# A hybrid decoder layer on one core: row scale into class order earlier, a pair's second turn later in its step, three weight tiles split in halves in other steps

## Chip, cores and metric

The kernel runs on one core of a Trainium2 chip. The metric is the device time of one execution in microseconds (us), as the median of several runs. Five engines work side by side, each through its own list of instructions in order: TensorE (PE, with its weight loads shown as PEld), VectorE (DVE), ScalarE (ACT), GpSimd (POOL) and SyncE (SP), which issues the DMAs here. An instruction that needs another engine's result waits on a semaphore, and what stands behind it on its engine waits with it.

## What is computed

One decoder layer on 1024 tokens of width 1024, in float32: attention over eight heads beside a gated recurrence over four heads, one output projection, and a feed-forward block.

```python
h = rmsnorm(x, mix_pre_norm[layer])
proj = h @ w_in[layer]
q_a, k_a, v_a, q_h, f_h, i_h, g_h = jnp.split(proj, splits, axis=-1)
attn = dilated_mixture_attention(q_a.reshape(ahead), k_a.reshape(ahead), v_a.reshape(ahead), slopes)
attn = rmsnorm(attn.reshape(B, S, ATTN_WIDTH), attn_out_norm[layer])
rec = hgrn2_recurrence(q_h, f_h, i_h, g_h, lower_bounds[layer], hgrn_out_norm[layer])
mixed = jnp.concatenate([attn, rec], axis=-1) @ w_out[layer]
x = x + rmsnorm(mixed, mix_post_norm[layer])
h = rmsnorm(x, mlp_pre_norm[layer])
ff = jnp.square(jax.nn.relu(h @ w_ff1[layer])) @ w_ff2[layer]
x = x + rmsnorm(ff, mlp_post_norm[layer])
```

The attention mixes three patterns with dilations 1, 4 and 16. The kernel therefore orders the tokens of a block by their class modulo 4 (`DIL = 4`) where it gathers keys by stride.

## The kernel before

Every matrix product runs in three passes (`three_pass`, L89 to L92): each operand is split into a rounded part `h` and a remainder `l`, and the products hh, hl and lh are added up in one PSUM bank. So each weight tile of 128 x 1024 must be split before use. `w_split` (L110) does it whole: ACT writes the rounded part (L86, or L124 with a gain for the output projection) and DVE the remainder (L87 or L125). `wo_half` (L132) does one half of 512 columns of an output tile (L140 on ACT, L141 on DVE); its second half also issues the next weight load on SP (L107). `w_get(i, ahead)` splits tiles in order until tile `i + ahead` is done. The raw tiles have two buffers, so a load can go out only when a split has freed one. The output projection has eight tiles, `WO0` to `WO0 + 7`; the first two take slabs of their own (tag S and BT, L179), the next two the ordinary weight buffers.

The order of the work is written out by hand: each engine executes its instructions in the order in which the Python code issues them. Projections are generators in a queue; `fill` (L195) takes units from it, mostly one contraction step of three matmuls of 128 x 512, and so sets the projections between the steps of the other work.

Two stretches matter here.

**The last recurrence heads and the first attention projections.** `rrow` (L253, 128 x 1024) holds the row scale of the first norm along the tokens, the same on all partitions. The recurrence heads use it in token order: `hgrn_qf` (L417) multiplies the projected q (L428) and the forget gate (L443) with it, for each half `hf` of 512 tokens, and then makes the gate's products (L444 to L452). The attention uses it in class order (L717, L781, L800). Between the two, ACT brings each half into class order with two copies, one with a strided read into a half-width buffer `rc` (L774) and one back (L775). Before, both pairs stand in `attn_proj(0)` (L758), each two contraction steps into the query projection of its half; the split of the next weight tile (`w_get` at `n == 4` of the first half) comes between them. The projection units of one recurrence head run inside `hgrn_core` (L484) of the head before: with the last gate products (L443 to L452) go the output sums of that head (L626 to L631), whose root POOL takes (L82, L83) before DVE applies the gate (L642). In the last head's core, the level loop multiplies keys and queries by running products (L580, L582 on DVE), and the next level's TensorE product `pl` (L576) reads them. Half-width buffers (tag `half`) come two at a time.

**The 64 attention steps.** The loop at L1326 makes eight steps for each of eight heads: four near blocks D0 to D3, two far pieces F0, F1, two pieces N0, N1. In a step, exponentials are taken on ACT (`raise_`, L936), the next scores are made (`look`), the step's weights are turned by TensorE transposes into a PSUM bank of tag t (`turn`, pt_D, pt_F, pt_N) and split from there by ACT and DVE (L975, L976), some projection units are filled in, the weights of the step before are multiplied with the values (`weigh`, pov), results are added up (`finish`, L1046), a key job follows in some steps (`key_job`, L736 on ACT, L737 on POOL), and then `hooks` (L1294) run what a step has of its own. More projection units end the step. Two heads make a pair. A finished pair's output is turned to token order in two parts: `pair_turn` (L1069) makes four transposes into a t bank (pot), and `pair_rows` (L1077) scales them out of the bank on DVE (L1079). The first part stands at the end of steps 17, 33 and 49, the second in steps 18, 34 and 50, with its transposes right behind the step's own `turn`. There are two banks of tag t.

The splits of the first output tiles stand at steps 42 (tile one, at the end of the step), 44 (tile two), 45 (tile three), 48 and 49 (tile four in halves). `row_turn` (L1146, transposes pmt, splits emt at L86 and L87) prepares token rows for the output projection, and from step 47 on `early_out` (L1173 on, product pwe) fills the projection units.

Of the kernel before, what the change touches and what calls it, by code (L numbers as in the profile page):

```python
# [11 lines left out]
AF = mybir.ActivationFunctionType  # L12
# [13 lines left out]
AH = 8  # L26
HH = 4
LEVELS = (1, 2, 4, 8, 16, 32, 64)
DIL = 4
# [3 lines left out]
def f32(ap):  # L33
    return ap.bitcast(F32)
# [3 lines left out]
def hymba_layer(ctx, tc, x, w_in, w_out, w_ff1, w_ff2, g_pre, lb_logits, g_mix, g_post,  # L38
                g_mlp, g_mlp_post, bias_tab, level_masks, ident_in, fold_in, out):
    nc = tc.nc  # L40
    V, S, G, TE = nc.vector, nc.scalar, nc.gpsimd, nc.tensor
# [18 lines left out]
    def half(name, dtype=F32):  # L60
        return sp.tile([P, 512], dtype, tag="half", name=name, bufs=2)
# [86 lines left out]
    def w_get(i, ahead=1):  # L148
        while done[1] < min(i + 1 + ahead, len(stream)):
            w_split()  # L150
        return parts[i]
# [26 lines left out]
    WO0 = len(stream)  # L178
# [13 lines left out]
    queue = []  # L192
# [17 lines left out]
    def drain():  # L210
        while queue:
            n = len(queue)
            fill(1e9)
            assert len(queue) < n or not queue
# [27 lines left out]
    for c in range(2):  # L242
        sl = slice(c * 512, c * 512 + 512)
# [150 lines left out]
    def classes(ap):  # L394
        return ap.rearrange("p (m r) -> p r m", r=DIL)
# [21 lines left out]
    def hgrn_qf(h):  # L417
        hd = heads[h]
        box = [None]
        w = w_get(4 * h + 2)  # L420
        qt = hd["qt"] = slab("S", f"qt{h}")
        sig = slab("P", f"sig{h}")
        for hf in range(2):
            sl = slice(hf * 512, hf * 512 + 512)
            yield from proj_t(w, f"q{h}", hf, box)
            if h == 0:
                row_scale(hf)
            V.tensor_tensor(out=qt[:, sl], in0=box[0], in1=rrow[:, sl], op=ALU.mult)  # L428
            S.activation(sig[:, sl], qt[:, sl], AF.Sigmoid)
            V.tensor_tensor(out=qt[:, sl], in0=qt[:, sl], in1=sig[:, sl], op=ALU.mult)  # L430
            yield 650.0
        w = w_get(4 * h + 3, 0)
        hd["prod"] = prod = [slab("BT", f"pr{q}{h}", F32R) for q in "hl"]
        kt = hd["kt"] = slab("S", f"kt{h}")
        tot = hd["tot"] = slab("S", f"tot{h}")
        for hf in range(2):
            sl = slice(hf * 512, hf * 512 + 512)
            for n, cost in enumerate(proj_t(w, f"f{h}", hf, box)):
                if hf == 0 and n == 3:
                    w_get(4 * h + 3, 2 if h + 1 < HH else 1)  # L440
                yield cost
            fr = half(f"fr{h}{hf}")
            V.tensor_tensor(out=fr, in0=box[0], in1=rrow[:, sl], op=ALU.mult)  # L443
            S.activation(tot[:, sl], fr, AF.Sigmoid)  # L444
            S.activation(kt[:, sl], fr, AF.Sigmoid, scale=-1.0)
            V.tensor_scalar(tot[:, sl], tot[:, sl], omlb[:, h:h + 1], lb[:, h:h + 1], op0=ALU.mult, op1=ALU.add)
            V.tensor_scalar(kt[:, sl], kt[:, sl], omlb[:, h:h + 1], None, op0=ALU.mult)
            full = half(f"pr{h}{hf}")
            V.tensor_tensor(out=full, in0=qt[:, sl], in1=kt[:, sl], op=ALU.mult)
            S.activation(prod[0][:, sl], full, AF.Copy)  # L450
            V.tensor_tensor(out=qt[:, sl], in0=qt[:, sl], in1=tot[:, sl], op=ALU.mult)
            V.tensor_tensor(out=prod[1][:, sl], in0=full, in1=f32(prod[0][:, sl]), op=ALU.subtract)  # L452
            yield 650.0

    def quarter_sets(hd, h, step, tots):

# [301 lines left out]
    def attn_proj(pr):  # L758
        stacks = [{}, {}]
        box = [None]  # L760
        while pr > 1 and not second_done[pr - 2]:
            yield None
        w = w_get(A0 + 3 * pr, 0)
        for hf in range(2):
            sl = slice(hf * 512, hf * 512 + 512)
            for n, cost in enumerate(proj_t(w, f"aq{pr}", hf, box)):
                if hf == 0 and n == 3 and turn_later:
                    values_turn()
                    cost += 450.0
                if hf == 0 and n == 4:  # L770
                    w_get(A0 + 3 * pr)
                if pr == 0 and n == 2:
                    moved = half(f"rc{hf}")
                    S.activation(moved.rearrange("p (r m) -> p r m", r=DIL), classes(rrow[:, sl]), AF.Copy)  # L774
                    S.activation(rrow[:, sl], moved, AF.Copy)  # L775
                yield cost
            if hf == 0:
                for i in range(2):
                    stacks[i]["q"] = slab("S", f"q{pr}_{i}", F32R)
            full = half(f"qf{pr}{hf}")  # L780
            V.scalar_tensor_tensor(full.rearrange("p (r m) -> p r m", r=DIL), classes(box[0]), -0.125,  # L781
                                   rrow[:, sl].rearrange("p (r m) -> p r m", r=DIL), op0=ALU.mult, op1=ALU.mult)
            lo = half(f"ql{pr}{hf}", F32R)
            for i, (a, b) in enumerate(halves):
                src = full[a:b].rearrange("p (r j i) -> p j r i", r=DIL, i=32)
                S.activation(by_class(stacks[i]["q"][a:b, sl]), src, AF.Copy)  # L786
                G.tensor_tensor(out=by_class(lo[a:b]), in0=src, in1=by_class(f32(stacks[i]["q"][a:b, sl])), op=ALU.subtract)  # L787
            nc.sync.dma_start(out=f32(stacks[0]["q"][64:128, sl]), in_=f32(lo[0:64]))
            nc.sync.dma_start(out=f32(stacks[1]["q"][0:64, sl]), in_=f32(lo[64:128]))
            yield 650.0  # L790
        wv = w_get(A0 + 3 * pr + 1, 0)
        vs = None

        def values(hf):
            for n, cost in enumerate(proj_t(wv, f"av{pr}", hf, box)):
                if n == 4:
                    w_get(A0 + 3 * pr + 1 + hf)
                yield cost
            full = half(f"vf{pr}{hf}")
            V.tensor_tensor(out=by_class(full), in0=in_blocks(box[0]),  # L800
                            in1=rrow[:, hf * 512:hf * 512 + 512].rearrange("p (r j i) -> p j r i", r=DIL, i=32), op=ALU.mult)
            turn_later.append((pr, vs, full, hf))
            yield 650.0

        vs = slab("V8", f"v{pr}", F32R, (P, NT, 2, 2, 64))
        yield from values(0)
        while pr > 0 and not first_done[pr - 1]:
            yield None
        wk = w_get(A0 + 3 * pr + 2, 0)
        for i in range(2):  # L810
            stacks[i]["kh"] = slab("S", f"kh{pr}_{i}", F32R)
            stacks[i]["kl"] = slab("S", f"kl{pr}_{i}", F32R)
        pairs[pr] = (stacks, vs)
        for hf in range(2):
            for n, cost in enumerate(proj_t(wk, f"ak{pr}", hf, box)):
                if n == 3 and hf == 0:
                    values_turn()
                    cost += 450.0
                yield cost
            keys_read(pr, box[0], hf)  # L820
            if hf == 0 and pr == AH // 2 - 1:
                early_rows()
            yield 650.0
        yield from values(1)
# [9 lines left out]
    def load_bias(hd):  # L834
        if hd < AH and hd not in bts:
            bts[hd] = slab("BT", f"bt{hd}") if hd < AH - 1 else early["table"][:, 0]
            nc.sync.dma_start(out=bts[hd][:, :NEAR + FAR], in_=table_dram[hd])
# [257 lines left out]
    NE = 4  # L1095
# [14 lines left out]
    def early_sums():  # L1110
        early["sum"] = [wide.tile([P, 2, D], F32, tag="A", name=f"esum{q}") for q in range(NE // 2)]
# [173 lines left out]
    for h in range(HH):  # L1285
# [10 lines left out]
        1: lambda: last_gate(1),  # L1296
        2: lambda: last_gate(2),
        3: lambda: last_gate(3),
        44: lambda: w_get(WO0 + 1, 0),
        45: lambda: w_split(),  # L1300
        46: lambda: row_turn(0, 0, tag="s"),
        47: lambda: [drain(), early_sums(), queue.extend(early_out(t) for t in range(NE))],
        48: lambda: [values_turn("t"), wo_half(3, 0)],
        49: lambda: [wo_half(3, 1), load_bias(AH - 1)],
        50: lambda: row_turn(1, 0),
        52: lambda: row_turn(2, 0),
        54: lambda: row_turn(3, 0),
        55: lambda: [wo_half(4, 0), row_load(0)],
# [17 lines left out]
    for s in range(n_steps):  # L1326
# [14 lines left out]
        if i == 2:  # L1341
            joint(hd, 0)
            spread_low(hd, 1)
        kind, g = ITEMS[i]
        turn(hd, kind, g)
        raise_(*coming, which=(1,))
        if s % 16 == 2 and s > 16:
            pair_turn(s // 16 - 1, 1)
        if kind != "D" or g % 2:
            to_weigh.append((hd, kind, g // 2 if kind == "D" else g))  # L1350
        units = UNITS[hd][i]
# [5 lines left out]
        for *w, r in last_fold:  # L1357
            finish(*w, *r)
        if s % 16 == 2 and s > 16:
            pair_rows(s // 16 - 1, 1)  # L1360
        if i == 0:
            far_queries(hd)
# [4 lines left out]
            send(hd)  # L1367
        elif i == 6:
            receive(hd)
        if s == 42:  # L1370
            w_get(WO0, 0)
        if i in (1, 2, 3, 6, 7):
            key_job()
        hooks.get(s, lambda: None)()
# [913 lines left out]
```

## Time and profile before

| | |
|---|---|
| median of three runs | 1212.91 us (1212.48 to 1214.87) |
| the profiled execution | 1212.77 us, its span 1211.0 us |
| granted TensorE clock | 0.999 |
| DMA, share of 16 engines | 43.8% |
| L774, class copy with strided read, 128 x 512 | 1.09 to 1.16 us, two of them |
| L775, copy back | 0.63 us, two of them |
| L124, whole output tile on ACT | 1.13 to 1.15 us |
| L140, half an output tile on ACT | 0.71 to 0.72 us |
| L141, the same half on DVE | 0.75 us |
| L1079, a pair's half scaled out of its bank | 0.68 to 0.69 us, six of them |

The span is the time from the first to the last instruction of the profiled execution; what lies around it belongs to the measured time as well. In the timeline a row gives the start and the duration in us, then engine, line, operation and tiles (out<-in); a bracket gives the engine's idle time before the instruction and what ended it. Instructions overlap a little at their ends, so the time that one holds its engine is best read from start to start.

### The profile page before, as it was taken

To read this page: it belongs to the slowest core of one execution; us is meant where nothing else is said; L and a number is where in the kernel's file an instruction comes from. 1 tells how busy PE (TensorE), PEld (TensorE's weight loads), DVE (VectorE), ACT (ScalarE), POOL (GpSimd) and SP (SyncE) were. 2 spreads that over 40 slices of the span, in tenths; PEclk is the share of its full clock that TensorE was granted. 3 is DMA by queue.
4 is the path that set the end of the run, shared out by engine and by line. 5 is a ranking of instruction groups with operands and counts; after the bars stand their busy time and mean duration, and the time that the engine had idled before them with its cause. 6 is when DMAs were issued, how large, how long until landed. Compare 5 with 4: busy or idle time off the path is not lost.

```text
span 1211.0 us, 17270 instructions
## 1 busy us (share of the span) xinstructions
PE 1197.1 (99%) x6338; PEld 1025.0 (85%) x6338; DVE 854.5 (71%) x1436; ACT 548.9 (45%) x1073; POOL 306.9 (25%) x288
## 2 busy tenths in 40 slices
PE   9999999999999999999999999999999999999997
PEld 8898989888888887888888888888888888888886
DVE  5697878776666767676689566766688554478796
ACT  7633333332565667765664222222234543534562
POOL 0121212021221211144330886575631000000022
PEclk9999999999999999999999999999999999999999
DMA  5222323123545456173514555554587534533337
GB/s 219 69 69 83 94 86 94 50 82 76 148 92 126 113 129 167 42 238 125 191 61 157 182 187 196 196 188 143 202 320 268 203 98 146 162 100 104 105 105 278
DMA packets 87667, 172.38 MB, mean 142 GB/s; under 512 B 14624, under 2 KB 40224, under 8 KB 87584
## 3 DMA queue, kind: packets, MB, share of 16 engines
q1 hardware_dynamic: 87584, 171.29, 43.8%
q8 instruction: 50, 0.82, 0.3%
q14 instruction: 33, 0.27, 0.1%
HBM read 116.98 MB, written 47.99 MB: 136 GB/s over the span
## 4 chain that ended last, share of the span: by engine, by line
PE 75%; ACT 1%; DVE 1%; issue 1%; POOL 0%; DVEq 0%; POOLq 0%; ACTq 0%
PE f L2028 18%; PE f2s L2028 7%; PE pwo L90 2%; PE pwo L92 2%; PE pwo L91 2%; PE pm_ak L90 1%; PE pm_av L90 1%; PE pm_ak L92 1%; PE pm_ak L91 1%; PE pm_av L92 1%; PE pm_av L91 1%; PE pm_aq L90 1%; PE pl L576 1%; PE pm_aq L92 1%; PE pm_aq L91 1%; PE pov L994 1%
## 5 line engine op out<-in xcount | busy, mean ns | idle before, releaser
L87 DVE TENSOR_TENSOR al<-ar,ah 128x1024 fp32r<-128x1024 f32 x56 | 70.6, 1261 | 80.9 <-ACT ah L86 78.6
L2028 PE MATMUL f<-bh,ah 128*128 128x512 f32 x320 | 124.5, 389 | 0.0
L2028 PE MATMUL f<-bl,ah 128*128 128x512 f32 x320 | 124.5, 389 | 0.0
L2028 PE MATMUL f<-bh,al 128*128 128x512 f32 x320 | 124.5, 389 | 0.0
L86 ACT ACTIVATE ah<-ar 128x1024 fp32r<-128x1024 f32 x56 | 59.2, 1057 | 86.0 <-DMA ar<-actd 85.7
L2028 PEld LDWEIGHTS f<-bh,ah 128*128 128x128 f32 x320 | 60.1, 188 | 12.6
L2028 PEld LDWEIGHTS f<-bl,ah 128*128 128x128 f32 x320 | 60.1, 188 | 12.5
L2028 PEld LDWEIGHTS f<-bh,al 128*128 128x128 f32 x320 | 60.1, 188 | 12.3
L2102 POOL TENSOR_SCALAR lbl<-ssq 128x1 f32<-128x1 f32 x4 | 3.3, 820 | 245.8 <-ACT fd L2098 245.6
L1651 POOL TENSOR_TENSOR e<-x,e 128x512 f32<-128x512 f32 x14 | 21.6, 1540 | 131.0 <-DVE x L1602 131.0
L2028 PE MATMUL f2s<-bh,al 128*128 128x512 f32 (+1 forms) x128 | 48.9, 382 | 0.0
L2028 PE MATMUL f2s<-bl,ah 128*128 128x512 f32 (+1 forms) x128 | 48.9, 382 | 0.0
L2028 PE MATMUL f2s<-bh,ah 128*128 128x512 f32 (+1 forms) x128 | 48.9, 382 | 0.0
L701 POOL TENSOR_SCALAR tout<-traw 128x256 f32<-128x256 f32 x16 | 18.4, 1149 | 107.7 <-DMA traw<-in_bias_tab_dram 99.9
L737 POOL TENSOR_TENSOR kl<-kf,kh 64x512 fp32r<-64x512 f32 x16 | 21.7, 1353 | 88.0 <-ACT kh L736 47.5
L87 DVE TENSOR_TENSOR bl<-br,bh 128x1024 fp32r<-128x1024 f32 x32 | 40.1, 1253 | 0.5 <-ACT bh L86 0.4
L2045 ACT ACTIVATE acc<-f 128x512 f32<-128x512 f32 x28 | 16.7, 598 | 49.7 <-PE f L2028 49.7
L787 POOL TENSOR_TENSOR ql<-qf,q 64x512 fp32r<-64x512 f32 x16 | 21.3, 1331 | 64.6 <-ACT q L786 55.3
L86 ACT ACTIVATE bh<-br 128x1024 fp32r<-128x1024 f32 x32 | 33.6, 1051 | 4.3 <-PE f L2028 2.9
L87 DVE TENSOR_TENSOR wl<-raw,wh 128x1024 fp32r<-128x1024 f32 x21 | 26.2, 1250 | 11.0 <-ACT wh L86 11.0
L90 PE MATMUL pwo<-woh,mt 128*128 128x512 f32 x80 | 32.2, 402 | 0.0
L92 PE MATMUL pwo<-woh,mt 128*128 128x512 f32 x80 | 31.2, 390 | 0.0
(1722 smaller groups left out, 3964.9 us busy)
## 6 DMA issues: line engine op xcount, KB each, us to landing
ar<-actd SPq DMA_DIRECT2D x56, 512.0 KB, 3.6
br<-in_w_ff_dram SPq DMA_DIRECT2D x16, 1024.0 KB, 6.0
w1r<-in_w_ff_dram SPq DMA_DIRECT2D x14, 1024.0 KB, 6.5
raw<-in_w_in_dram SPq DMA_DIRECT2D x26, 512.0 KB, 3.7
actd<-e SPq DMA_DIRECT2D x17, 768.0 KB, 4.4
actd<-e SPq DMA_DIRECT2D x11, 1024.0 KB, 4.1
raw<-in_w_out_dram SPq DMA_DIRECT2D x8, 512.0 KB, 4.5
xres<-in_x_dram SPq DMA_DIRECT2D x8, 512.0 KB, 4.0
```

The source lines that it names most:

```text
L86: S.activation(hi, src, AF.Copy)
L87: eng.tensor_tensor(out=lo, in0=src, in1=f32(hi), op=ALU.subtract)
L90: TE.matmul(dst, lhs[0], rhs[0], start=start, stop=False)
L91: TE.matmul(dst, lhs[0], rhs[1], start=False, stop=False)
L92: TE.matmul(dst, lhs[1], rhs[0], start=False, stop=stop)
L576: TE.matmul(pl[:, n * 64:(n + 1) * 64], kt[:, n * P:(n + 1) * P], qv[:, n * nb:(n + 1) * nb, 1, :], start=True, stop=True)
L701: G.tensor_scalar(by_class(dst[:, part_ * w:(part_ + 1) * w]), in_blocks(raw[:, FAR * DIL:]), -1.0, None, op0=ALU.mult)
L737: G.tensor_tensor(out=kl[a:b], in0=src, in1=f32(kh[a:b]), op=ALU.subtract)
L787: G.tensor_tensor(out=by_class(lo[a:b]), in0=src, in1=by_class(f32(stacks[i]["q"][a:b, sl])), op=ALU.subtract)
L1651: eng[0].tensor_tensor(out=e1[:, 3], in0=a21, in1=e1[:, 2], op=ALU.add)
L2028: TE.matmul(pm, a[:, j, c], b[:, j, d], start=start and j == 0 and q == 0, stop=stop and j == 1 and q == 2, skip_group_check=True)
L2045: S.activation(acc_at(p, i), pm, AF.Copy)
```

## The change

Three things move; nothing is computed otherwise.

- The two class copies become a function. The first half's pair is issued by the last recurrence head, behind the gate products of its first half, and the second half's pair in the first attention projection at `n == 5` of the first half, one contraction step behind the weight split.
- `pair_turn(..., 1)` moves from behind the step's own turn to behind the filled units, the weighing and `finish`, right in front of `pair_rows(..., 1)`.
- Tile one's split moves from the end of step 42 to ahead of that step's turn. Tile two is split in halves in steps 43 and 45 instead of whole in 44, tile three in halves in steps 46 and 47 instead of whole in 45, and tile four's second half goes from step 49 to step 50.

```diff
             V.tensor_tensor(out=prod[1][:, sl], in0=full, in1=f32(prod[0][:, sl]), op=ALU.subtract)
+            if h == HH - 1 and hf == 0:
+                rrow_by_class(0)
             yield 650.0
+
+    def rrow_by_class(hf):
+        sl = slice(hf * 512, hf * 512 + 512)
+        moved = half(f"rc{hf}")
+        S.activation(moved.rearrange("p (r m) -> p r m", r=DIL), classes(rrow[:, sl]), AF.Copy)
+        S.activation(rrow[:, sl], moved, AF.Copy)
...
                 if hf == 0 and n == 4:
                     w_get(A0 + 3 * pr)
-                if pr == 0 and n == 2:
-                    moved = half(f"rc{hf}")
-                    S.activation(moved.rearrange("p (r m) -> p r m", r=DIL), classes(rrow[:, sl]), AF.Copy)
-                    S.activation(rrow[:, sl], moved, AF.Copy)
+                if pr == 0 and hf == 0 and n == 5:
+                    rrow_by_class(1)
                 yield cost
...
-        44: lambda: w_get(WO0 + 1, 0),
-        45: lambda: w_split(),
-        46: lambda: row_turn(0, 0, tag="s"),
-        47: lambda: [drain(), early_sums(), queue.extend(early_out(t) for t in range(NE))],
+        43: lambda: wo_half(1, 0),
+        45: lambda: wo_half(1, 1),
+        46: lambda: [row_turn(0, 0, tag="s"), wo_half(2, 0)],
+        47: lambda: [wo_half(2, 1), drain(), early_sums(), queue.extend(early_out(t) for t in range(NE))],
         48: lambda: [values_turn("t"), wo_half(3, 0)],
-        49: lambda: [wo_half(3, 1), load_bias(AH - 1)],
-        50: lambda: row_turn(1, 0),
+        49: lambda: load_bias(AH - 1),
+        50: lambda: [wo_half(3, 1), row_turn(1, 0)],
...
         if i == 2:
             joint(hd, 0)
             spread_low(hd, 1)
+        if s == 42:
+            w_get(WO0, 0)
         kind, g = ITEMS[i]
         turn(hd, kind, g)
         raise_(*coming, which=(1,))
-        if s % 16 == 2 and s > 16:
-            pair_turn(s // 16 - 1, 1)
...
         if s % 16 == 2 and s > 16:
+            pair_turn(s // 16 - 1, 1)
             pair_rows(s // 16 - 1, 1)
...
-        if s == 42:
-            w_get(WO0, 0)
         if i in (1, 2, 3, 6, 7):
             key_job()
         hooks.get(s, lambda: None)()
```

## The prediction

> **What bounds the kernel now.** I read the page's first lines first, then TensorE's row of the view of waits, then the busy times by stretch.
>
> ```profile
> span 1211.0 us, 17270 instructions
> PE 1197.1 (99%) x6338; PEld 1025.0 (85%) x6338; DVE 854.5 (71%) x1436; ACT 548.9 (45%) x1073; POOL 306.9 (25%) x288
> ```
>
> ```profile
> PE pot L1075 <- DVE anat L1079: 1.8, 2, 1.5
> PE pl L576 <- DVE qt L582: 1.2, 1, 1.2
> ```
>
> ```profile
> 240.00:283.00 43.00, 41.19 (x235) 35.30 (x233) 30.77 (x46) 13.68 (x19) 10.62 (x8) 1.00 0.32 83
> ...
> 449.00:462.00 13.00, 12.20 (x75) 10.11 (x74) 9.29 (x26) 10.29 (x27) 3.53 (x3) 1.00 0.47 102
> 462.00:480.00 18.00, 16.52 (x111) 14.49 (x110) 15.18 (x45) 11.67 (x29) 1.29 (x1) 1.00 0.60 153
> ...
> 600.00:900.00 300.00, 300.00 (x1328) 248.16 (x1327) 216.08 (x227) 97.58 (x124) 169.91 (x110) 1.00 0.50 179
> ```
>
> TensorE is busy for 99% of the span, and the change removes no matmul. All it can bring is TensorE's idle time in three places. The columns of a stretch are its length, then the busy time of PE, PEld, DVE, ACT and POOL, then clock and DMA. PE lacks 1.81 us of 43 around the class copies, 0.80 of 13 and 1.48 of 18 around the first weight splits of the output projection; 600 to 900 us show no gap. DMA waits are no part of it. The idle time that a row prints starts at a matmul's modelled end, which overlaps its successor, so below I count from where the next one was due: matmuls of 512 columns follow at 0.23 us, transposes at 0.11.
>
> **Part 1: the row scale in class order.**
>
> ```profile
> 238.85 0.63 ACT L450 ACTIVATE prh<-pr 128x512 fp32r<-128x512 f32 x1 [1.28 <-DVE pr L449]
> ...
> 239.38 0.58 ACT L630 ACTIVATE ysq<-po 128x512 f32<-128x512 f32 x1
> ...
> 241.06 0.60 ACT L630 ACTIVATE ysq<-po 128x512 f32<-128x512 f32 x1 [1.10 <-PE po L628]
> ...
> 250.32 0.69 DVE L452 TENSOR_TENSOR prl<-pr,prh 128x512 fp32r<-128x512 f32 x1
> ...
> 251.71 1.09 ACT L774 ACTIVATE rc<-rrow 128x512 f32<-128x512 f32 x1
> ...
> 251.79 0.40 PE L493 MATMUL pd<-prl,ones 128*128 128x512 f32 x1
> ...
> 252.84 0.63 ACT L775 ACTIVATE rrow<-rc 128x512 f32<-128x512 f32 x1
> ...
> 253.38 1.04 ACT L86 ACTIVATE wh<-raw 128x1024 fp32r<-128x1024 f32 x1
> ...
> 254.45 1.23 DVE L87 TENSOR_TENSOR wl<-raw,wh 128x1024 fp32r<-128x1024 f32 x1 [3.44 <-ACT wh L86]
> ...
> 258.84 1.76 DVE L582 TENSOR_TENSOR qt<-qt,tot 128x512 f32<-128x512 f32 x1
> ...
> 259.08 0.39 PE L92 MATMUL pm_av<-hTh,wl 128*128 128x512 f32 x1
> ...
> 260.66 2.00 PE L576 MATMUL pl<-qt,kt 128*128 128x64 f32 x16 [1.18 <-DVE qt L582]
> ```
>
> The level product pl was due at 259.31 and came at 260.66: 1.35 us lost. It waits for DVE's L582, and from DVE's L87 on that engine runs without a pause; L87 waits for ACT's L86, and L86 stands behind the two class copies, which hold ACT from 251.71 to 253.38 = 1.67 us. The change takes that pair from in front of L86. But it puts the first pair behind the first L450, in front of L630, where ACT is not idle: L630 starts at 239.38 + 1.67 = 241.05, and the second L630, now back to back with it, at about 241.60 instead of 241.06. That 0.55 goes through the sums, POOL's root and the gate into the last L450 and L452, and so into the table load ahead of L86. I take 0.6: L86 starts at 251.71 + 0.6 = 252.3 instead of 253.38, 1.07 sooner, and L582 ends as much sooner, at 259.5. The wait shrinks from 1.35 to about 0.28: **gain 1.07 us**. Bounds: 0.3, if the late chain costs more, and 1.35, if pl is no longer late at all. L452 would end at 251.61 instead of 251.01; the last pd matmul wants it at 251.79, so this cover is 0.2 us, and whatever lateness goes beyond it is lost. The second pair now runs behind L86, beside L87 and L781 on DVE, and ends near 255.0, just ahead of L786, whose input comes at 255.2: hidden. Neither pair issues a DMA. The short buffers (two of them) change hands in another order; each earlier reader ends by then, POOL's L787 last, so I cost that at nothing.
>
> **Part 2: the pair's second turn.**
>
> ```profile
> 369.08 0.49 PE L946 MATMUL pt_D<-ident,pd 128*128 128x128 f32 x3
> ...
> 369.85 0.66 PE L1075 MATMUL pot<-ident,o 128*128 128x128 f32 x4 [0.28 <-DVE anat L1079]
> ...
> 372.24 0.68 DVE L1079 TENSOR_TENSOR anat<-pot,rd 128x512 f32<-128x512 f32 x1
> ...
> 423.19 0.49 PE L946 MATMUL pt_D<-ident,pd 128*128 128x128 f32 x3
> ...
> 423.71 0.66 PE L1075 MATMUL pot<-ident,o 128*128 128x128 f32 x4
> ...
> 424.99 0.68 DVE L1079 TENSOR_TENSOR anat<-pot,rd 128x512 f32<-128x512 f32 x1
> ...
> 474.50 0.49 PE L946 MATMUL pt_D<-ident,pd 128*128 128x128 f32 x3
> ...
> 476.47 0.66 PE L1075 MATMUL pot<-ident,o 128*128 128x128 f32 x4 [1.48 <-DVE anat L1079]
> ```
>
> pot takes the t bank that the first turn filled, so it waits until DVE's L1079 has read it. Three transposes take 0.33, so pot was due at 369.41, 423.52 and 474.83: 0.44, 0.19 and 1.64 us lost. Moved behind a projection unit (3 x 0.23) and the weighting's four matmuls (0.5), it comes 1.1 to 1.2 us later in TensorE's order, and the bank is free. DVE's second L1079 now waits for pot: in steps 18 and 34 DVE reached it at 372.24 and 424.99, and pot would be read out at about 371.3 and 425.3, so at most 0.3 of DVE's time with nothing urgent behind it (L781 and key copies). **Gain 0.44 + 0.19 = 0.63 us**; step 50 is summed in part 3. No instruction is added, and L1079's four DMAs keep their place on SP. Bounds 0 and 0.63.
>
> **Part 3: the output tiles' splits.**
>
> ```profile
> 450.89 0.49 ACT L975 ACTIVATE pth<-pt_D 128x384 fp32r<-128x384 f32 x1 [1.97 <-PE pt_D L946]
> ...
> 452.40 1.15 ACT L124 ACTIVATE woh<-raw,gcols 128x1024 fp32r<-128x1024 f32 x1
> ...
> 453.31 0.63 PE L946 MATMUL pt_D<-ident,pd 128*128 128x128 f32 x4
> ...
> 454.69 0.58 ACT L975 ACTIVATE pth<-pt_D 128x512 fp32r<-128x512 f32 x1
> ...
> 455.75 0.44 PE L958 MATMUL pt_F<-ident,pf 128*128 128x128 f32 x2 [0.31 <-ACT pf L936]
> ...
> 457.74 0.70 PE L958 MATMUL pt_F<-ident,pf 128*128 128x128 f32 x3
> ...
> 458.37 1.15 ACT L124 ACTIVATE woh<-raw,gcols 128x1024 fp32r<-128x1024 f32 x1
> ...
> 461.40 0.44 PE L955 MATMUL pt_N<-ident,pn 128*128 128x128 f32 x2 [0.49 <-ACT pn L936]
> ...
> 470.91 0.71 ACT L140 ACTIVATE wh<-raw,gcols 128x512 fp32r<-128x512 f32 x1
> ...
> 474.94 0.75 DVE L141 SCALAR_TENSOR_TENSOR wl<-raw,gcols,wh 128x512 fp32r<-128x512 f32 x1
> ...
> 477.27 0.55 DVE L976 TENSOR_TENSOR ptl<-pt_D,pth 128x384 fp32r<-128x384 f32 x1
> ...
> 478.07 0.62 PE L1159 MATMUL pmt<-ident,erows 128*128 128x128 f32 x4
> ```
>
> ACT is the late engine from 452.4 to 461.4: TensorE loses 0.47 at 455.28 (the pt_F transpose due there started at 455.75), 0.21 at 457.74 (0.70 for three instead of 0.49) and 0.68 before 461.40. Tile one's split moves ahead of step 42's turn, into the 1.97 us in which ACT idled; its slabs fall free with the last look of the step, near 450.5, so L975 slips to about 451.6 and DVE's share of that turn to 453.4, which nothing wants before 455.2. The next L975 then starts when its transposes end, 453.31 + 0.63 = 454.0, 0.7 sooner: the first wait goes. But half a tile now stands in step 43; it holds ACT for 0.61. What comes before the second pt_F is thus only 0.1 sooner, and the wait there grows to about 0.6. With tile two's 1.06 gone from step 44, the exponentials of step 46's pt_N end near 460.2, ahead of TensorE: that wait goes. By step 46 the gain is 0.1 + 0.68 = 0.78.
>
> In step 50 the 1.64 goes, and what is late next is pmt: it takes the bank of pt_D, which DVE's L976 must have read. L976 ended at 477.82; with everything 0.78 sooner and one L141 (0.75) taken out from before it, it ends at 476.3. pmt would be due at 478.07 - 0.78 - 1.64 = 475.65, so it waits some 0.65 and comes at 476.3: **gain 1.77 us** for this part with step 50. The second half of tile four lands behind L1079 and in front of the next emt; it is wanted 0.4 us after it ends. The raw loads behind tiles two to four go out up to 2 us later on SP; the least cover is that of tile four, some 4 us. Bounds: 0 (ACT as late as now) and 3.0 (0.47 + 0.21 + 0.68 + 1.64, no new wait).
>
> Splitting two more tiles costs ACT 2 x 0.71 - 1.15 = 0.27 each, in a stretch where it is busy 10.29 of 13 us. The Trainium skill, "Perfetto Trace Analysis", section Optimizing Scalar/DVE Operations, advises larger operations where an engine is saturated and breaking them up where it is not saturated but makes others wait. Read by its first half, with the 0.54 put on the path, the total below would be 3.0 instead of 3.5; by its second half it stays.
>
> **Sum.** 1.07 + 0.63 + 1.77 = 3.5 us. The profiled execution took 1212.77 (span 1211.0 and 1.8 around it), 0.14 below the median of 1212.91. After it TensorE has no wait of size that a shift could lengthen, so the gain stays: span 1207.5, **median 1209.4 us**.
>
> **Rivals.**
> - *All waits go* (L452's lateness does not reach L86; L976 comes in time): 1.35 + 0.63 + 3.0 = 5.0, 1207.9 us. For it: each engine has idle time nearby. Against: the halves' 0.61 in step 43. Chance 0.12.
> - *ACT stays the bound*: if tile one's slabs come free only near 452, the split delays L975 instead of filling a gap, the half in step 43 adds to it, and part 3 keeps only step 50's share, about 1; with 0.3 for part 1 and 0.3 for part 2 that is 1.6: 1211.3 us. ACT's 79% in that stretch speaks for it, the 1.97 idle against. Chance 0.24.
> - *The moves do nothing*: DVE is late at the new places by as much. 1212.9 us, chance 0.04.
> - *Slower, by the granted clock*: TensorE without its gaps might be granted less. A thousandth of clock costs 1.2 us over the whole span, so below 0.996 it outweighs 3.5 us; at 0.995, against the 1.00 of the stretches above, 1214.3 us. Against it: 300 us without a gap ran at 1.00. Chance 0.05. The Trainium skill, "TensorE: Matmul & The Clock Gate", section on the HAM clock gate, puts a lower full-load clock down to three busy cores of a die; only one runs here.
>
> **Range and chances.** The forecast as summed, with a gain of 2.4 to 4.5, has 0.55. The range, 1207.5 to 1211.7, holds it, the first rival and most of the second. About 0.2% (2.4 us) is what a measurement of this kernel can tell from no change: faster 0.67, same 0.28, slower 0.05.
>
> **What would show it.** Right: pl near 259.6 with a wait below 0.4; pot without a wait in all three places; pt_N without one; a pt_F wait of about 0.6 in step 45 and a pmt wait of about 0.6 in step 50. Wrong: L630 not later (then part 1 is larger), a pd matmul that waits for L452, the first L124 still after L1001, a wait of pwe for L141, or a clock below 1.00.

## The result and the profile after

| | before | after |
|---|---|---|
| median of 7 runs each (us) | 1213.03 (1212.48 to 1214.87) | 1209.36 (1208.67 to 1210.08) |
| profiled execution (us) | 1212.77 | 1210.08 |
| its span (us) | 1211.0 | 1208.2 |

The ratio is 0.9968, with a 95% interval of 0.9956 to 0.9979: 3.7 us faster, or 2.5 to 5.3 by the interval. The first lines of the page of after, and lines of TensorE from its view of waits (engine, line and tile, what was waited for, then us in all, times, longest):

```profile
span 1208.2 us, 17277 instructions
...
PE 1197.4 (99%) x6338; PEld 1026.5 (85%) x6338; DVE 853.9 (71%) x1438; ACT 548.8 (45%) x1075; POOL 309.4 (26%) x288
```

```profile
...
PE pl L584 <- DVE tot L594: 0.6, 1, 0.6
PE pmt L1165 <- DVE ptl L982: 0.5, 1, 0.5
PE pt_F L964 <- ACT pf L942: 0.5, 1, 0.5
...
PE pl L584 <- DVE qt L590: 0.2, 1, 0.2
```

Line numbers have moved: the class copies are L460 and L461, pl is L584 (was L576), its producer L590 (L582), pot L1081 (L1075), pmt L1165 (L1159), pt_F L964 (L958). The two waits that the prediction set out to remove, pot 1.8 and pl on qt 1.2 in the list of before, are gone, or in pl's case down to 0.2; pmt is new and pt_F has grown. The same stretches as before, with the same columns:

```profile
240.00:283.00 43.00, 42.22 (x243) 36.27 (x242) 31.67 (x47) 14.34 (x21) 10.64 (x8) 1.00 0.32 83
449.00:462.00 13.00, 12.47 (x82) 10.90 (x82) 10.40 (x26) 10.85 (x33) 2.57 (x2) 1.00 0.45 97
462.00:480.00 18.00, 17.46 (x118) 15.46 (x116) 15.06 (x46) 13.11 (x35) 1.69 (x2) 1.00 0.64 166
600.00:900.00 300.00, 300.00 (x1329) 248.19 (x1328) 214.99 (x230) 97.93 (x123) 167.31 (x107) 1.00 0.51 180
```

TensorE now lacks 0.78, 0.53 and 0.54 us where it lacked 1.81, 0.80 and 1.48, and the granted clock is 1.00 throughout.

The two spans can't simply be subtracted. Near 5 us eight warm-up matmuls took 1.89 us in the profiled execution of before and 3.14 in this one, and the first matmul of the attention's query projection, ahead of every wait that the change touches, stands at 244.30 in the timeline of before and at 245.18 here:

```profile
5.01 3.14 PE L314 MATMUL pig<-warm 128*128 128x256 f32 x8
...
245.18 0.39 PE L90 MATMUL pm_aq<-hTh,wh 128*128 128x512 f32 x1
```

So this execution carries 0.88 us from its start. In what follows a gain is the shift of the same matmuls between two timelines, less the shift of that first pm_aq. The last matmul of the kernel stands at 1204.65 before and at 1201.86 after: 2.79 + 0.88 = **3.67 us**. The difference of the medians is the same figure, which is chance to the hundredth, given their interval. By place it is 1.05 behind pl, 1.56 behind step 18's pot, 1.83 behind step 34's, 2.61 behind step 46 and 3.65 behind step 50.

**Part 1.** ACT's, DVE's and TensorE's timelines of after (start, duration, engine, line, operation, out<-in):

```profile
240.26 1.14 ACT L460 ACTIVATE rc<-rrow 128x512 f32<-128x512 f32 x1
241.44 0.63 ACT L461 ACTIVATE rrow<-rc 128x512 f32<-128x512 f32 x1
241.97 1.07 ACT L638 ACTIVATE ysq<-po 128x512 f32<-128x512 f32 x2
...
253.21 1.04 ACT L86 ACTIVATE wh<-raw 128x1024 fp32r<-128x1024 f32 x1
```

```profile
257.22 1.52 DVE L588 TENSOR_TENSOR kt<-kt,tot 128x512 f32<-128x512 f32 x1
258.67 1.78 DVE L590 TENSOR_TENSOR qt<-qt,tot 128x512 f32<-128x512 f32 x1
```

```profile
259.95 0.39 PE L92 MATMUL pm_av<-hTh,wl 128*128 128x512 f32 x1
260.50 2.00 PE L584 MATMUL pl<-qt,kt 128*128 128x64 f32 x16 [0.16 <-DVE qt L590]
```

Less 0.88, the squares (L638) begin at 241.09, the weight split (L86) at 252.33 and L590 ends at 259.57. pl, at 260.50 (259.62 less 0.88), is 0.16 sooner than before in the plain timeline and so 1.04 sooner without the late start (1.05 behind it). It follows its predecessor by 0.55 where 0.23 was due: 0.32 of the wait is left.

**Part 2.** pot in steps 18 and 34, TensorE's timeline of after:

```profile
370.35 0.62 PE L1081 MATMUL pot<-ident,o 128*128 128x128 f32 x4
...
423.95 0.62 PE L1081 MATMUL pot<-ident,o 128*128 128x128 f32 x4
```

No wait stands at either. The gain grows by 0.51 and 0.27: 0.78 together.

**Part 3 and step 50.** ACT's, then TensorE's, then DVE's timeline:

```profile
447.87 1.14 ACT L124 ACTIVATE woh<-raw,gcols 128x1024 fp32r<-128x1024 f32 x1
449.94 0.49 ACT L981 ACTIVATE pth<-pt_D 128x384 fp32r<-128x384 f32 x1 [0.93 <-PE pt_D L952]
...
454.49 0.71 ACT L140 ACTIVATE woh<-raw,gcols 128x512 fp32r<-128x512 f32 x1
...
456.38 0.46 ACT L942 ACTIVATE pf<-pf,stat 128x192 f32<-128x192 f32 x1
```

```profile
456.18 0.27 PE L964 MATMUL pt_F<-ident,pf 128*128 128x128 f32 x1
456.98 0.44 PE L964 MATMUL pt_F<-ident,pf 128*128 128x128 f32 x2 [0.53 <-ACT pf L942]
...
459.48 0.62 PE L961 MATMUL pt_N<-ident,pn 128*128 128x128 f32 x4
...
472.70 0.50 PE L952 MATMUL pt_D<-ident,pd 128*128 128x128 f32 x3
472.95 0.48 PE L90 MATMUL pwe<-wh,emt 128*128 128x512 f32 x1
...
474.14 0.62 PE L1081 MATMUL pot<-ident,o 128*128 128x128 f32 x4
475.30 0.66 PE L1165 MATMUL pmt<-ident,erows 128*128 128x128 f32 x4 [0.54 <-DVE ptl L982]
```

```profile
474.69 0.55 DVE L982 TENSOR_TENSOR ptl<-pt_D,pth 128x384 fp32r<-128x384 f32 x1
475.16 0.68 DVE L1085 TENSOR_TENSOR anat<-pot,rd 128x512 f32<-128x512 f32 x1
```

Tile one is split directly behind the exponentials of step 42, in ACT's idle time, and L981 still waits 0.93 for TensorE behind it. The half of tile two at 454.49 stands in front of the exponential at 456.38, for which the second transpose of its pt_F group waits: the second starts 0.80 after the first, where 0.11 was due. pt_N has no wait. In step 50 pot has none, and pmt waits for DVE's L982, which ends at 475.24. From the F pieces to step 46 the gain grows by 0.78, in step 50 by 1.04; with 0.02 behind it Part 3 gives 1.84. The three parts, 1.05 + 0.78 + 1.84, make the 3.67.

### The profile page after: what moved, and what is told of

Read it like the earlier page. It is cut to its first block, busy times and chain, and to the rows that moved or that the text cites. A ratio compares the mean times of both kernels' runs of the same rounds, so it can differ in the third digit from the quotient of the medians.

```text
span 1208.2 us, 17277 instructions
## 1 busy us (share of the span) xinstructions
PE 1197.4 (99%) x6338; PEld 1026.5 (85%) x6338; DVE 853.9 (71%) x1438; ACT 548.8 (45%) x1075; POOL 309.4 (26%) x288
## 4 chain that ended last, share of the span: by engine, by line
PE 93%; DVE 2%; ACT 2%; issue 1%; DMA 0%; POOL 0%; SPq 0%; DVEq 0%; POOLq 0%; ACTq 0%
PE f L2033 18%; PE f2s L2033 7%; PE pig L92 2%; PE pig L90 2%; PE pig L91 2%; PE pl L520 2%; PE pwo L90 2%; PE pwo L92 2%; PE pwo L91 2%; PE pm_ak L90 1%; PE pm_av L90 1%; PE pm_ak L92 1%; PE pm_ak L91 1%; PE pm_av L92 1%; PE pm_av L91 1%
## 5 line engine op out<-in xcount | busy, mean ns | idle before, releaser
L86 ACT ACTIVATE ah<-ar 128x1024 fp32r<-128x1024 f32 x56 | 59.1, 1056 | 88.0 <-DMA ar<-actd 87.6
L745 POOL TENSOR_TENSOR kl<-kf,kh 64x512 fp32r<-64x512 f32 x16 | 21.3, 1330 | 86.3 <-ACT kh L744 70.0
L793 POOL TENSOR_TENSOR ql<-qf,q 64x512 fp32r<-64x512 f32 x16 | 21.3, 1331 | 62.6 <-ACT q L792 62.0
L86 ACT ACTIVATE bh<-br 128x1024 fp32r<-128x1024 f32 x32 | 33.6, 1051 | 3.9 <-PE f L2033 3.0
```

The costliest lines, as they stand in the source:

```text
L86: S.activation(hi, src, AF.Copy)
L745: G.tensor_tensor(out=kl[a:b], in0=src, in1=f32(kh[a:b]), op=ALU.subtract)
```

## The experiments

Ratios are to before, timed beside them on the same chip: its median was 1213.7 (29 runs) beside the first four kernels (11, 11, 11 and 7 runs) and 1214.07 (9 runs) beside the last four, which ran on another chip (5 runs each).

| kernel | median (us) | ratio to before, 95% |
|---|---|---|
| rowscale_only | 1212.21 | 0.9986 (0.9977 to 0.9995) |
| turn_only | 1212.93 | 0.9993 (0.9985 to 1.0002) |
| splits_only | 1211.58 | 0.9984 (0.9975 to 0.9993) |
| tile_one_only | 1210.59 | 0.9973 (0.9962 to 0.9984) |
| half_in_42 | 1209.24 | 0.9960 (0.9948 to 0.9973) |
| copy_after_sums | 1208.93 | 0.9959 (0.9947 to 0.9972) |
| rows_end_of_50 | 1208.66 | 0.9956 (0.9943 to 0.9970) |
| all_three | 1207.65 | 0.9948 (0.9935 to 0.9960) |

The intervals are 2 to 3 us wide and several effects are smaller, so the places decide. (By the medians the last four stand 4.8 to 6.4 us below before, by the timelines 4.1 to 5.3; the last section comes back to how widely the runs of before spread.) This table has the gain on before in us, by one profiled execution of each: the median shift of the same matmuls in the 4 us from 268, 380, 435, 470 and 490 of before's timeline, and of the last one, each less the first pm_aq's shift.

| kernel | behind pl | behind step 18 | behind step 34 | behind step 46 | behind step 50 | end |
|---|---|---|---|---|---|---|
| after | 1.05 | 1.56 | 1.83 | 2.61 | 3.65 | 3.67 |
| rowscale_only | 1.05 | 1.07 | 1.07 | 1.07 | 1.06 | 1.07 |
| turn_only | -1.61 | -1.09 | -0.82 | -0.83 | -0.67 | -0.71 |
| splits_only | -0.02 | -0.02 | -0.02 | 0.74 | 1.37 | 1.40 |
| tile_one_only | 1.03 | 1.55 | 1.83 | 2.50 | 2.66 | 2.52 |
| half_in_42 | 1.06 | 1.57 | 1.85 | 3.25 | 4.27 | 4.12 |
| copy_after_sums | 1.45 | 1.97 | 2.25 | 3.02 | 4.06 | 4.10 |
| rows_end_of_50 | 1.06 | 1.57 | 1.85 | 2.61 | 4.32 | 4.29 |
| all_three | 1.45 | 1.95 | 2.23 | 3.62 | 5.33 | 5.29 |

### Each part alone

**The class copies alone.**

```diff
+            if h == HH - 1 and hf == 0:
+                rrow_by_class(0)
...
-                if pr == 0 and n == 2:
...
+                if pr == 0 and hf == 0 and n == 5:
+                    rrow_by_class(1)
```

> The class copies moved, nothing else. Theory: pl of the second level, counted from the first projections on (where the executions are alike again), comes 1.0 us sooner than before and still waits 0.3; the gain stays to the end: 1.0 us against before. Rival (the later output sums cost as much as the copies gave): a pd matmul waits for prl and less than 0.3 us is gained. Rival (the copies were the whole delay): 1.35 us, no wait of pl.

The gain is 1.05 behind pl and 1.07 at the end. The view of waits of this kernel no longer has pl behind qt, and keeps pot:

```profile
PE pot L1081 <- DVE anat L1085: 1.8, 2, 1.5
```

Part 1 is worth about 1 us, and none of it is given back later.

**The second turn alone.**

```diff
         raise_(*coming, which=(1,))
-        if s % 16 == 2 and s > 16:
-            pair_turn(s // 16 - 1, 1)
...
         if s % 16 == 2 and s > 16:
+            pair_turn(s // 16 - 1, 1)
             pair_rows(s // 16 - 1, 1)
```

> Only the pair's second turn moved. Theory: the waits of pot in steps 18 and 34 go, 0.8 us together; in step 50 pot waits little, but pmt behind it waits about 1 us for the bank that DVE's L976 has yet to read, since DVE is as late as before, so step 50 gives only 0.2: 1.0 us in all. Rival (the place of the turn is the whole of step 50's wait): 0.8 + 1.6 = 2.4 us.

The 1.61 lost at pl is a dip of the granted clock, told of in the last section. From there steps 18 and 34 gave 0.52 and 0.27, step 50 only 0.16 of the 1.64 that stood there, 0.9 to the end. TensorE's timeline of this kernel in step 50 shows why:

```profile
477.82 0.66 PE L1075 MATMUL pot<-ident,o 128*128 128x128 f32 x4 [0.37 <-DVE anat L1079]
479.23 0.66 PE L1159 MATMUL pmt<-ident,erows 128*128 128x128 f32 x4 [0.76 <-DVE ptl L976]
```

The wait has been divided: pot still waits 0.4 for L1079, and then pmt waits 0.8 for L976, both of them DVE instructions in one order with the splits. A turn that stands later in TensorE's order helps little while DVE is late.

**The splits alone.**

```diff
-        44: lambda: w_get(WO0 + 1, 0),
-        45: lambda: w_split(),
-        46: lambda: row_turn(0, 0, tag="s"),
+        43: lambda: wo_half(1, 0),
+        45: lambda: wo_half(1, 1),
+        46: lambda: [row_turn(0, 0, tag="s"), wo_half(2, 0)],
...
+        if s == 42:
+            w_get(WO0, 0)
         kind, g = ITEMS[i]
         turn(hd, kind, g)
```

> Only the output tiles' splits moved. Theory: 0.7 to 0.8 us by step 46; in step 50 pot stands right behind the turn as before and still waits, about 0.9 instead of 1.64, because DVE's L1079 comes sooner without a split before it, and pmt then waits for nothing: 1.5 us in all. Rival (step 50's wait belongs to the turn's place alone): 0.8 us.

From step 34 to step 46 it gains 0.76, to the end 1.40. Its waits still have pot:

```profile
PE pot L1075 <- DVE anat L1079: 1.0, 2, 0.7
```

The longest is 0.7 here, against 1.5 before: taking an L141 out from before L1079 gives 0.63 of step 50's 1.04. The three parts alone add up to 1.07 + 0.9 + 1.40 = 3.37, 0.3 less than together. Most of that is step 50: the turn alone gains 0.16 there and the splits alone 0.63, together 1.04, since the turn and the split each need the other.

### Which of the splits counts

**After, with tiles two to four at their old places**, so that of the splits only tile one's moves (the class copies and the turn stay as in after):

```diff
-        43: lambda: wo_half(1, 0),
-        45: lambda: wo_half(1, 1),
+        44: lambda: w_get(WO0 + 1, 0),
+        45: lambda: w_split(),
...
-        50: lambda: [wo_half(3, 1), row_turn(1, 0)],
+        50: lambda: row_turn(1, 0),
```

> The changed kernel with tiles two to four split where they were before; only tile one's move, the class copies and the turn are kept. Theory: by step 46 as much is gained as with the halves (0.7 us), because the half in step 43 gives back what it takes from step 44; in step 50 the split ahead of L1079 keeps DVE late, pmt waits about 0.9 and the kernel ends 0.9 us behind the changed one, at a gain of 2.8 against before. Rival (two instructions instead of one cost ACT 0.27 us a tile in a full stretch): 0.5 us faster than the changed one.

It ends 1.15 behind after by the timelines and 1.2 behind by the medians, of separate sets of runs. Of its waits:

```profile
PE pmt L1165 <- DVE ptl L982: 0.8, 1, 0.8
...
PE pt_N L961 <- ACT pn L942: 0.5, 1, 0.5
PE pot L1081 <- DVE anat L1085: 0.4, 1, 0.4
```

pt_F's wait is away and pt_N's is back, so that behind step 46 it is only 0.11 behind after: among steps 43 to 47 it hardly matters where tiles two and three stand. In step 50 it gains 0.16 where after gains 1.04: there tile four's second half, in step 49, is what costs. In DVE's timeline of this kernel its L141 (0.75) starts at 472.45, in front of the L1085 and the L982 for which pot and pmt wait. The remaining 0.16 goes later, nearly all of it at a pt_F transpose near 506 and a pt_N transpose near 512.

This says little about halves against whole tiles. Tile four is split in halves in both kernels, and what step 50 shows is where its second half stands. For tiles two and three the two kernels are 0.11 apart behind step 46, although two halves take ACT 2 x 0.71 instead of 1.14. The Trainium skill ("Perfetto Trace Analysis", section Optimizing Scalar/DVE Operations) has advice for both sides, larger operations where an engine is saturated and breaking them up where it makes others wait; neither decides here, since no run has whole tiles and halves in the same places.

### The waits that are left

The prediction named three waits that would remain. Each got one edit to after.

**pt_F in step 45**: the half of tile two that stands in front of its exponentials moves to step 42, behind tile one.

```diff
-        43: lambda: wo_half(1, 0),
...
         if s == 42:
             w_get(WO0, 0)
+            wo_half(1, 0)
```

> The changed kernel with the first half of tile two split in step 42, behind tile one and ahead of the turn, instead of in step 43. Theory: the half in step 43 is what makes the second pt_F wait; ACT has about 0.9 us idle in step 42 to take it. The wait of 0.77 shrinks below 0.2 and the end comes 0.6 us sooner than with the changed kernel. Rival (ACT is full there in any order): the wait moves to pt_N in step 46, 0.2 us or less is gained.

ACT's timeline of this kernel shows the half behind the whole tile, the second pt_F group runs in one piece, and no pt_F stands among the waits:

```profile
447.26 1.14 ACT L124 ACTIVATE woh<-raw,gcols 128x1024 fp32r<-128x1024 f32 x1
448.30 0.71 ACT L140 ACTIVATE woh<-raw,gcols 128x512 fp32r<-128x512 f32 x1
```

```profile
455.57 0.61 PE L964 MATMUL pt_F<-ident,pf 128*128 128x128 f32 x3
```

Behind step 46 it is 0.64 ahead of after, at the end 0.45. The half in step 43 was the cause of that wait. The lead is still 0.62 behind step 50; then 0.2 goes back, at the same pt_F and pt_N near 506 and 512 as above. What holds these two was not tested.

**pl's last 0.3**: the first pair of copies moves behind the output sums, so that the squares don't wait for it.

```diff
-            if h == HH - 1 and hf == 0:
-                rrow_by_class(0)
...
+        if h == HH - 2:
+            rrow_by_class(0)
```

> The changed kernel with the first pair of class copies behind both squares of the recurrence's output sums (where ACT is idle) instead of in front of the first. Theory: the squares, the gate, the last gate products and the table load come 0.6 us sooner, so does the weight split, and pl waits for nothing: 0.3 us sooner than the changed kernel. Rival (the table load or another wait holds the split): no change, pl still waits 0.3.

```profile
252.59 1.04 ACT L86 ACTIVATE wh<-raw 128x1024 fp32r<-128x1024 f32 x1
```

```profile
260.19 1.89 PE L582 MATMUL pl<-qt,kt 128*128 128x64 f32 x16
```

L86 starts 0.62 sooner than in after (253.21), from the same start, and pl 0.31 sooner, now without a wait; behind pl the lead is 0.40 and at the end 0.43. So the first pair made L86 late by the 0.6 that the prediction charged for it, and a part of that was slack.

**pmt in step 50**: its `row_turn` goes to the end of the step.

```diff
-        50: lambda: [wo_half(3, 1), row_turn(1, 0)],
+        50: lambda: wo_half(3, 1),
...
+        if s == 50:
+            row_turn(1, 0)
```

> The changed kernel with the row transposes pmt of step 50 behind the step's last projection unit instead of right behind pot. Theory: pmt's wait is for the bank that L982 reads; a unit later the bank is free, the wait of 0.6 to 0.8 goes and nothing takes its place, since emt was early enough: 0.6 us sooner than the changed kernel. Rival (the lateness moves on): the turn of step 51 or the first product on emt waits instead, no gain.

Behind step 50 it is 0.67 ahead of after, at the end 0.62, and pmt has left the list of waits.

**All three edits together.**

> The changed kernel with all three of these: the half in step 42, the class copy behind the squares, the rows at the end of step 50. Theory: the three add up, 1.5 us sooner than the changed kernel, 5.1 us against before. Rival (the waits trade places): no more than 0.8 us sooner than the changed kernel.

Its waits in full:

```profile
PE xt L290 <- DMA xr<-in_x_dram: 1.8, 1, 1.8
PE pig L314 <- DVE nhalf L252: 1.4, 1, 1.4
PE pl L582 <- DVE tot L592: 0.6, 1, 0.6
PE pig L337 <- ACT wig0h L86: 0.5, 1, 0.5
PE pd L1035 <- DVE stat L889: 0.2, 1, 0.2
PE pov_far L1022 <- DVE ptNl L982: 0.2, 1, 0.2
```

Against after it leads by 0.40 behind pl, 1.01 behind step 46, 1.68 behind step 50 and 1.62 at the end, and the end is 5.29 sooner than before. xt and the two pig waits belong to the start; behind it 1.0 us of waits is left. Its median of 1207.65 is below those of both kernels, 1.7 us below after's, which comes from another set of runs.

## Why the prediction was right

- **Part 1 right, 1.07 against 1.05.** Squares at 241.09 (predicted 241.05), L86 at 252.33 (252.3), the end of L590 at 259.57 (259.5), 0.32 of wait left (0.28). copy_after_sums shows the charge for the first pair by itself. No pd matmul waited for L452.
- **Part 2 too small, 0.63 against 0.78.** The mechanism held: pot waits at neither place. What was mis-sized is the time that pot's wait cost, by 0.07 and 0.08. Three transposes were charged 0.33 before pot was due, and in the timeline above the matmul behind three of them follows after 472.95 - 472.70 = 0.25, which would make the gains 0.52 and 0.27. But that matmul then holds TensorE for 0.31 (the next one starts at 473.26) where 0.23 is usual, so this reading of the 0.08 is not shown.
- **Part 3 right in size, 1.77 against 1.84 (0.78 by step 46, as measured), with one step wrong.** "Its slabs fall free with the last look of the step, near 450.5, so L975 slips to about 451.6" did not happen: the split began at 447.87, directly behind the exponential in front of it, and L981 went on waiting for TensorE. In the times of before, to which 450.5 belongs, that is 447.87 - 0.88 + 1.83 = 448.82 (1.83 us had been gained by then): the slab of the rounded part was free 1.7 us sooner than assumed, at the least. It cost the sum nothing, since the prediction took the delayed turn as wanted by nobody before 455.2. The rest came as charged: a wait of 0.8 - 0.11 = 0.69 in front of the second pt_F transpose (0.6), none at pt_N, none at pot in step 50, and pmt 0.78 later than pot's group (474.14 to 475.30, less 0.38 for the four transposes) would have put it (0.65).
- **The sum.** It was 3.47, and the places give 3.67. That the median still came out at 1209.36 for a forecast of 1209.4 is in part luck: the forecast started from a median of 1212.91, and before's median beside after was 1213.03.
- **The rivals.** *All waits go* failed at the two places that the prediction held against it: the half in step 43, and L976 (now L982). all_three reaches the 5 us of that rival, by three more moves. *ACT stays the bound* rested on the slabs; they were free. *The moves do nothing* lies outside the interval. *The granted clock* stayed at 0.999 in all seven runs of after.

## What to carry to other kernels

Where one engine is 99% busy, go through its waits one by one: reckon from when the next instruction was due, follow the releaser back to the instruction that stands in front of it on its own engine, and ask what is late next, because a removed wait is worth only its distance to that. A wait that two engines share needs both orders changed, as in step 50: the turn alone or the split alone gave part of it. After such a change, read the list of waits again: the remaining three took three small moves and gave another 1.6 us.

## What was not expected of the hardware

**Behind a wait of just over a microsecond the clock can fall.** In the profiled execution of turn_only pl waits for L582 as in before, and behind it TensorE's timeline has matmuls of 512 columns at 0.43 us instead of 0.23:

```profile
261.20 2.20 PE L576 MATMUL pl<-qt,kt 128*128 128x64 f32 x16 [1.20 <-DVE qt L582]
...
263.73 0.63 PE L91 MATMUL pm_av<-hTl,wh 128*128 128x512 f32 x1
264.16 0.63 PE L92 MATMUL pm_av<-hTh,wl 128*128 128x512 f32 x1
```

Its stretches, whose third number from the end is the granted clock, against 1.00 in the same stretch of before:

```profile
262.00:265.00 3.00, 3.00 (x15) 2.63 (x15) 3.00 (x5) 1.89 (x4) 0.78 (x1) 0.64 0.53 144
265.00:270.00 5.00, 5.00 (x29) 4.37 (x28) 3.45 (x3) 0.87 (x1) 2.25 (x2) 0.87 0.33 66
```

In finer windows the clock is 1.00 from 259.4 to 262.8, 0.50 from 262.9 to 266.2 and 1.00 again from 266.4: the dip lasts about 3.4 us, and it puts everything behind it 1.6 us later (the first column of the table above). The profiled executions of before and splits_only have the same wait, 1.18 and 1.20 us, and no dip behind it. The Trainium skill, "TensorE: Matmul & The Clock Gate", Part 1 on the HAM clock gate, gives half the clock after an idle window of about 3.4 us; the rate agrees, but TensorE had idled for 1.2 us only. From 259.4 to 262.8 it was busy for 2.20 us, most of that with the sixteen small matmuls of pl; whether they count as well isn't shown.

On the chip of the first four kernels the runs of turn_only fall into two groups: five executions at a mean clock of 0.997 took 1213.4 to 1214.3 us, the six others, at 0.998 or 0.999, 1211.8 to 1212.9. A mean of 0.998 alone is no sign of a dip: all_three's profiled execution has it with the clock at 1.00 until its last matmul has started, at 1199.93, and at 0.50 from 1202.6 us to the end. The spread of the times tells more. Where pl has its wait of 1.2 us (before in each set, turn_only, splits_only), the 7 to 29 runs of one kernel spread over 2.0 to 3.6 us; where the wait is gone or at most 0.2 (after and the six other kernels), its 5 to 11 runs spread over 0.5 to 1.4. So Part 1 may be worth more than its 1.05 us in the mean of many runs. That the dip comes from pl's wait is argued from one profile and these spreads, and not shown.

**DVE beside POOL.** L588 and L590 took 1.52 and 1.78 us in the rows of Part 1, and 0.67 and 0.68 one level later (262.70 and 263.30 in DVE's timeline of after). Beside the slow pair POOL runs L793:

```profile
256.90 2.99 POOL L793 TENSOR_TENSOR ql<-qf,q 64x512 fp32r<-64x512 f32 x2 [11.01 <-ACT q L792]
```

The Trainium skill, "SBUF — State Buffer", section Who interferes with whom, has a DVE instruction with two SBUF inputs contend with a POOL instruction that reads SBUF; these rows agree. Of the seven such pairs between 257 and 290 us in the timeline of after, three start while a POOL instruction runs, and they take 1.52 to 1.54 and 1.78 us; the other four start beside none and take 0.67 to 0.69 each. The same slow pair stands in before (L580 and L582, 1.53 and 1.76), and as an estimate from these rows, start to start, it takes some 1.9 us more than a fast one. That is more than the 1.35 us that pl was late there: beside the class copies it is a second way to that wait, and an untested one. The pl wait of 0.6 that is left in all_three has the same pattern (L586 and L588 at 1.54 and 1.77 beside POOL's L745). That moving the POOL work would end it wasn't tried.
